# Streamed weight tiles of two kinds written at byte 192 of their buffers instead of byte 0

## The chip, the cores and the metric

The kernel runs on one core of one Trainium2 chip. The metric is device time in microseconds (us) of one execution. Before the change the median of 3 runs is 396.92 us (396.71 to 397.27).

## The reference

Two layers of a decoder trunk, batch 1, 256 rows of 1024 features, float32. Cut to what matters here:

```
for l in range(2):
    h = rms_norm(x, norm_g[l])
    proj = h @ w_in[l]                       # 1024 -> 10 groups of 512 columns
    q_a, k_a, v_a, q_h, f_h, i_h, q_m, z = split(proj)
    o_a = moba_attention(rope(norm(q_a)), rope(norm(k_a)), v_a)
    o_h = rms_norm(hgrn2_chunkwise(q_h, f_h, i_h, lb[l]))
    kv_m = rms_norm(mem, mem_norm_g[l]) @ w_mem_kv[l]      # 1024 -> 2 * 512 columns
    o_m = memory_attention(norm(q_m), norm(k_m), v_m)
    y = concat(o_a, o_h, o_m) * silu(z)
    x = x + y @ w_out[l]                     # 1536 -> 1024
```

The three kinds of large product (`h @ w_in`, `mem @ w_mem_kv`, `y @ w_out`) are nearly all of the arithmetic.

## The kernel before

**One stream of weights.** The weights of both layers come as 120 chunks of 128 partitions x 1024 float32 in a fixed list (`chunks`). For each chunk SyncE loads the raw tile `wr` (4 buffers); ScalarE writes `wh`, a copy in fp32r, the reduced 4-byte matmul format (`h_to`, line 143, or line 148 with a gain for the memory chunks; 4 buffers); VectorE writes the rest `wl` = `wr` - `wh` (`l_to`, line 158 or 161; 3 buffers). Activations are split into a high and a low part in the same way (`hTh`, `hTl` in the tile `hT`; `mTh`, `mTl`; `yh`, `yl`), and each product is made of three matmuls: high x high, high x low and low x high. `slot` asks for loads, high parts and low parts a set number of chunks ahead of TensorE. Small work (norms, attention, the recurrence) runs as generators that `step` moves on between the pieces of a group; its matmuls stand between the large ones on TensorE.

**Four kinds of chunk.** In a name such as `acc<-wh,hT` the profile puts the moving operand (the one that streams through TensorE) ahead of the stationary one (the one that a weight load, PEld, puts in place). In this document one matmul with its weight load is a step.

- "B" chunks, the row-output groups KA, QA, IH, ZH, QM and VA (`group_b`): the weights are the moving operand, 512 wide, and a 128x128 block of `hT` is stationary. 6 groups x 8 blocks of the depth x 2 row halves x 3 products x 2 layers = 576 steps.
- "K" chunks, the memory projections (`group_kv`): the same form with `mTh` or `mTl` stationary. 2 column halves x 8 x 2 x 3 x 2 layers = 192 steps (one of them is cut in two).
- "A" chunks in `group_a`, the column-output groups FH, QH, ZA and ZM: a 128x128 block of weights is stationary and `hT` is the moving operand, 256 wide. 768 steps.
- "A" chunks in `w_out_phase` (line 1213): weights stationary, `yh` or `yl` moving, 256 wide. 576 steps.

In each layer the order is K (layer 0: ahead of all; layer 1: right behind the output projection of layer 0), FH, QH (A), KA, QA, IH, ZH (B), ZA, ZM (A), QM, VA (B), then the output projection. So TensorE goes over from 512-wide steps to 256-wide ones and back several times in a layer.

**Where the tiles start.** Buffers of `wh` and `wl` are 1088 elements (4352 bytes, 17 x 256) wide, and 1024 elements of them are used. The first one used is number 16 (byte 64) for A chunks and number 0 for B and K chunks. In the built program all these buffers start at multiples of 256 bytes. Start bytes of matmul operands within a stretch of 256 bytes:

| steps | moving operand | stationary operand |
|---|---|---|
| A (`group_a`) | `hT`: 0 | `wh`, `wl`: 64 |
| output projection | `yh`, `yl`, `y`: 0 | `wh`, `wl`: 64 |
| B | `wh`, `wl`: 0 | `hT`: 0 |
| K | `wh`, `wl`: 0 | `mTh`, `mTl`: 0 |
| scores of the memory attention (line 1142, told as L198) | `kmh`, `kml`: 64 | `qmh`: 64, `qml`: 0 |

All large steps are recorded by the helper `mm` (line 198), so they are told apart by their tiles.

Of the kernel before, what the change touches and what calls it, by code (L numbers as in the profile page):

```python
# [46 lines left out]
def hymba_kernel(ctx: ExitStack, tc: tile.TileContext, front, x, x_t, mem, mem_t, positions, w_in, w_out, w_mem_kv,  # L47
# [40 lines left out]
    chunks = []  # L88
# [30 lines left out]
    def pin(ins):  # L119
        tc.keep_in_program_order(ins)  # L120
# [12 lines left out]
    def parts(i):  # L133
        return (slice(0, 512), slice(512, 1024)) if i < 3 else (slice(0, 1024),)

    def h_to(n):
        while st["h"] < min(n, len(chunks)):
            i = st["h"]
            off = 16 if chunks[i][0] == "A" else 0
            whs[i] = sb.tile([128, 1088], F32R, name="wh", tag="wh", bufs=WH_BUFS)[:, off:off + 1024]  # L140
            g = chunks[i][2]
            if g is None:
                ins = nc.scalar.copy(whs[i], raws[i])  # L143
                if i == 12:
                    pin(ins)
            else:
                for sl in parts(i):
                    nc.scalar.activation(whs[i][:, sl], raws[i][:, sl], AF.Copy, scale=gT[:, g:g + 1])  # L148
            st["h"] += 1

    def l_to(n):
        while st["l"] < min(n, len(chunks)):
            i = st["l"]
            off = 16 if chunks[i][0] == "A" else 0
            wls[i] = sb.tile([128, 1088], F32R, name="wl", tag="wl", bufs=WL_BUFS)[:, off:off + 1024]
            g = chunks[i][2]
            if g is None:
                nc.vector.tensor_tensor(wls[i], raws[i], whs[i].bitcast(F32), op=OP.subtract)  # L158
            else:
                for sl in parts(i):  # L160
                    nc.vector.scalar_tensor_tensor(wls[i][:, sl], in0=raws[i][:, sl], scalar=gT[:, g:g + 1],  # L161
                                                   in1=whs[i][:, sl].bitcast(F32),
                                                   op0=OP.mult, op1=OP.subtract)
            st["l"] += 1
# [24 lines left out]
    def slot(first):  # L189
        if first:  # L190
            c = st["c"]
            dma_to(c + 1 + DMA_AHEAD)
            h_to(c + 1 + H_AHEAD)
            l_to(c + 1 + L_AHEAD)
        step()
# [163 lines left out]
    m_split(0, 1)  # L359
    m_split(1, 2)  # L360
    h_to(1)
    l_to(1)
    h_to(2)
    l_to(2)

    rm = cst.tile([128, 2], F32, name="rm")
# [993 lines left out]
```

## Time and profile before

| | us |
|---|---|
| median of 3 runs (lowest, highest) | 396.92 (396.71, 397.27) |
| the profiled execution | 397.62 |
| its span in the trace | 395.8 |

The profiled execution is 1.8 us longer than its span, and 0.7 us above the median of the runs. The page gives the busy time of each engine, the chain of work that ended last, and groups of equal instructions with their busy time, the mean duration of one in ns and the idle time ahead of them. Durations of matmuls overlap, since they are pipelined; the pace is read from the start times of the timeline.

### The profile page before, as it was taken

What the parts mean: (1) busy time and instruction counts of PE and PEld (TensorE: products, weight loads), DVE (VectorE), ACT (ScalarE), POOL (GpSimd) and SP (SyncE); (2) the same over time, 40 slices, a digit from 0 to 9 for tenths busy, and PEclk for the clock granted to TensorE, in tenths of its full rate; (3) what the DMA queues carried; (4) which work ended last, traced back from release to release, by engine and by line L of the source; (5) the groups of instructions that cost most, each with busy time, mean ns of one, the idle gap of its engine ahead of it and who ended that gap; (6) DMA issues with size and microseconds to landing.
All of it is one profiled execution on the core that took longest, in us unless ns stands there. A gap on an engine that the chain in (4) does not pass through costs nothing.

```text
span 395.8 us, 7904 instructions
## 1 busy us (share of the span) xinstructions
PE 391.1 (99%) x3051; PEld 354.0 (89%) x3051; DVE 315.5 (80%) x628; ACT 249.6 (63%) x399; POOL 65.9 (17%) x94
## 2 busy tenths in 40 slices
PE   8999999999999999999999999999999999999996
PEld 5889988888999888999988999888889998899996
DVE  4699988999899848776586998699989695588553
ACT  6787765455959679644463775444696774977330
POOL 2005923650002002000061030042200100200000
PEclk9999999999999999999999999999999999999999
DMA  7998664368634454433646475464764346344203
GB/s 251 421 357 270 206 214 159 121 197 265 206 122 157 161 178 139 155 115 111 209 162 209 124 237 185 152 201 172 206 221 154 113 134 214 133 159 161 87 21 108
DMA packets 22662, 70.92 MB, mean 179 GB/s; under 512 B 2529, under 2 KB 5985, under 8 KB 22625
## 3 DMA queue, kind: packets, MB, share of 16 engines
q1 hardware_dynamic: 19872, 67.86, 50.8%
q10 hardware_dynamic: 2752, 2.56, 2.4%
q8 instruction: 24, 0.39, 0.4%
q14 instruction: 14, 0.11, 0.1%
HBM read 67.27 MB, written 1.05 MB: 173 GB/s over the span
## 4 chain that ended last, share of the span: by engine, by line
PE 98%; DMA 1%; SPq 0%; ACT 0%; DVE 0%; issue 0%; DVEq 0%
PE acc L198 61%; PE acc L1213 17%; PE sd L198 11%; PE sd L202 2%; PE sd L1087 1%; PE sd L1066 1%; DMA wr<-in_front_dram 1%; PE sd L981 1%; PE sd L1175 1%; PE sd L765 0%; PE sd L633 0%; PE sd L1121 0%; SPq L123 0%; ACT wh L148 0%; PE sd L423 0%; PE sd L460 0%
## 5 line engine op out<-in xcount | busy, mean ns | idle before, releaser
L143 ACT CAST wh<-wr 128x1024 fp32r<-128x1024 f32 x104 | 108.8, 1052 | 82.6 <-PE acc L198 45.9
L158 DVE TENSOR_TENSOR wl<-wr,wh 128x1024 fp32r<-128x1024 f32 x104 | 126.5, 1221 | 26.8 <-PE acc L1213 8.5
L198 PE MATMUL acc<-wh,hT 128*128 128x512 f32 x384 | 120.5, 392 | 0.0
L198 PE MATMUL acc<-hT,wh 128*128 128x256 f32 x512 | 91.1, 279 | 0.0
L198 PEld LDWEIGHTS acc<-wh,hT 128*128 128x128 f32 x384 | 72.0, 188 | 14.8
L198 PEld LDWEIGHTS acc<-hT,wh 128*128 128x128 f32 x512 | 78.1, 188 | 0.3
L198 PE MATMUL acc<-wl,hT 128*128 128x512 f32 x192 | 75.6, 394 | 0.0
L198 PE MATMUL acc<-hT,wl 128*128 128x256 f32 x256 | 70.9, 279 | 0.0
L198 PEld LDWEIGHTS acc<-hT,wl 128*128 128x128 f32 x256 | 48.1, 189 | 0.2
L198 PEld LDWEIGHTS acc<-wl,hT 128*128 128x128 f32 x192 | 36.1, 188 | 7.2
L1213 PE MATMUL acc<-yh,wl 128*128 128x256 f32 x128 | 35.7, 279 | 0.0
L1213 PE MATMUL acc<-yh,wh 128*128 128x256 f32 x128 | 35.5, 281 | 0.0
L1213 PE MATMUL acc<-yl,wh 128*128 128x256 f32 x128 | 35.4, 278 | 0.0
L1213 PEld LDWEIGHTS acc<-yl,wh 128*128 128x128 f32 x128 | 24.1, 189 | 0.1
L161 DVE SCALAR_TENSOR_TENSOR wl<-wr,gT,wh 128x1024 fp32r<-128x1024 f32 (+1 forms) x14 | 19.1, 1374 | 6.4 <-ACT wh L148 2.1
L1213 PEld LDWEIGHTS acc<-yh,wl 128*128 128x128 f32 x128 | 24.1, 188 | 0.0
L1213 PEld LDWEIGHTS acc<-yh,wh 128*128 128x128 f32 x128 | 24.0, 188 | 0.1
L148 ACT ACTIVATE wh<-wr,gT 128x1024 fp32r<-128x1024 f32 (+1 forms) x14 | 15.2, 1090 | 11.7 <-PE acc L198 3.6
L1213 PE MATMUL acc<-y,wh 128*128 128x256 f32 x128 | 21.8, 276 | 0.0
L1213 PEld LDWEIGHTS acc<-y,wh 128*128 128x128 f32 x128 | 19.2, 188 | 0.0
L1047 ACT ACTIVATE P<-P,nba,rq 128x256 f32<-128x256 f32 (+1 forms) x32 | 17.2, 539 | 0.9 <-DVE nba L1038 0.8
L1213 PE MATMUL acc<-y,wl 128*128 128x256 f32 x64 | 17.5, 276 | 0.0
(245 smaller groups left out, 667.5 us busy)
## 6 DMA issues: line engine op xcount, KB each, us to landing
wr<-in_w_in_dram SPq DMA_DIRECT2D x80, 512.0 KB, 3.7
wr<-in_w_out_dram SPq DMA_DIRECT2D x24, 512.0 KB, 3.2
wr<-in_w_mem_kv_dram SPq DMA_DIRECT2D x12, 512.0 KB, 3.3
k<-k ACTq DMA_DIRECT2D x8, 256.0 KB, 4.1
zT<-in_x_dram SPq DMA_DIRECT2D x2, 512.0 KB, 8.9
xs<-in_x_t_dram SPq DMA_DIRECT2D x2, 512.0 KB, 9.9
memr<-in_mem_dram SPq DMA_DIRECT2D x2, 512.0 KB, 5.7
mw<-in_front_dram SPq DMA_DIRECT2D x2, 384.0 KB, 5.8
```

The costliest lines, as they stand in the source:

```text
L143: ins = nc.scalar.copy(whs[i], raws[i])
L148: nc.scalar.activation(whs[i][:, sl], raws[i][:, sl], AF.Copy, scale=gT[:, g:g + 1])
L158: nc.vector.tensor_tensor(wls[i], raws[i], whs[i].bitcast(F32), op=OP.subtract)
L161: nc.vector.scalar_tensor_tensor(wls[i][:, sl], in0=raws[i][:, sl], scalar=gT[:, g:g + 1], in1=whs[i][:, sl].bitcast(F32), op0=OP.mult, op ...
L198: nc.tensor.matmul(o, lhsT=a, rhs=b, start=s, stop=e)
L202: tc.keep_in_program_order(nc.tensor.matmul(o, lhsT=a, rhs=b, start=True, stop=True))
L981: nc.tensor.transpose(pt[:, p * 128:(p + 1) * 128], kr[:, t, p * 128:(p + 1) * 128], ident)
L1047: pin(nc.scalar.activation(P[:, i, kc[t]], P[:, i, kc[t]], AF.Exp, bias=nb[:, c:c + 1], scale=rq[:, r:r + 1], accum_out=sm[:, c:c + 1]))
L1066: pin(nc.tensor.transpose(pt[:, i * 128:(i + 1) * 128], P[:, i, bs], ident))
L1087: pin(nc.tensor.matmul(po[w][rows, c + o:c + 256], lhsT=va[:, b, h * 64:(h + 1) * 64], rhs=PT[e][:, p, 256 * b:256 + 128 * b], start=b == ...
L1175: nc.tensor.transpose(pt[:, i * 256 + t * 128:i * 256 + (t + 1) * 128], P[:, t, i, b * 128:(b + 1) * 128], ident)
L1213: ins = nc.tensor.matmul(a, lhsT=wt, rhs=y, start=first and (to is not None or b % 2 == 0), stop=n == nk - 1 and j == 2, skip_group_check= ...
```

## The change

The offset into the buffer becomes 48 elements (byte 192) for B and K chunks; A chunks keep 16 (byte 64). Buffers, their sizes and their addresses are as before, and so is every instruction on every engine and its order: only the addresses that ScalarE and VectorE write to, and TensorE reads its moving operand from, are 192 bytes higher in the 48 B and 16 K chunks.

```
 def h_to(n):
...
-            off = 16 if chunks[i][0] == "A" else 0
+            off = 16 if chunks[i][0] == "A" else 48
             whs[i] = sb.tile([128, 1088], F32R, name="wh", tag="wh", bufs=WH_BUFS)[:, off:off + 1024]
...
 def l_to(n):
...
-            off = 16 if chunks[i][0] == "A" else 0
+            off = 16 if chunks[i][0] == "A" else 48
             wls[i] = sb.tile([128, 1088], F32R, name="wl", tag="wl", bufs=WL_BUFS)[:, off:off + 1024]
```

In the table of start bytes the moving operand of B and K steps goes from 0 to 192. Counted round a stretch of 256 bytes, the stationary operand then starts 64 bytes further on than the moving one in B and K steps, as it does in A steps and the output projection.

More of the change, by code (lines that the diff above doesn't have):

```diff
@@ L138, in h_to @@
             i = st["h"]
-            off = 16 if chunks[i][0] == "A" else 0
+            off = 16 if chunks[i][0] == "A" else 48
             whs[i] = sb.tile([128, 1088], F32R, name="wh", tag="wh", bufs=WH_BUFS)[:, off:off + 1024]
@@ L153, in l_to @@
             i = st["l"]
-            off = 16 if chunks[i][0] == "A" else 0
+            off = 16 if chunks[i][0] == "A" else 48
             wls[i] = sb.tile([128, 1088], F32R, name="wl", tag="wl", bufs=WL_BUFS)[:, off:off + 1024]
```

## The prediction

> **What bounds the kernel now.** I read the page's busy times and its chain first, then what TensorE waited for.
>
> ```profile
> span 395.8 us, 7904 instructions
> PE 391.1 (99%) x3051; PEld 354.0 (89%) x3051; DVE 315.5 (80%) x628; ACT 249.6 (63%) x399; POOL 65.9 (17%) x94
> PE 98%; DMA 1%; SPq 0%; ACT 0%; DVE 0%; issue 0%; DVEq 0%
> PE acc L198 <- ACT wh L148: 0.9, 1, 0.9
> PE sd L198 <- PEq L1349: 0.8, 1, 0.8
> ```
>
> TensorE is busy for 391.1 of 395.8 us, the chain runs through it for 98%, and it waits 1.7 us in all for others. So the time is the sum of the steps of TensorE, and an edit counts by what it does to the distance from one step's start to the next. Durations of steps overlap and don't tell that distance; the timeline does. First the A steps (256 wide, weights stationary) in two places of layer 0, with the last 512-wide step ahead of the first place:
>
> ```profile
> 28.30 0.40 PE L198 MATMUL acc<-wl,mTh 128*128 128x512 f32 x1
> 28.53 0.28 PE L198 MATMUL acc<-hT,wl 128*128 128x256 f32 x1
> 28.65 0.40 PE L198 MATMUL acc<-hT,wh 128*128 128x256 f32 x2
> 28.89 0.28 PE L198 MATMUL acc<-hT,wl 128*128 128x256 f32 x1
> ...
> 29.95 0.28 PE L198 MATMUL acc<-hT,wl 128*128 128x256 f32 x1
> ```
>
> ```profile
> 46.00 0.28 PE L198 MATMUL acc<-hT,wl 128*128 128x256 f32 x1
> 46.12 0.39 PE L198 MATMUL acc<-hT,wh 128*128 128x256 f32 x2
> 46.34 0.28 PE L198 MATMUL acc<-hT,wl 128*128 128x256 f32 x1
> ...
> 47.36 0.28 PE L198 MATMUL acc<-hT,wl 128*128 128x256 f32 x1
> ```
>
> Each triple (high x high, low x high, high x low) has one `hT,wl` step, so four triples, 12 steps, lie between the outer rows. The first place takes 29.95 - 28.53 = 1.42 us for them, 118.3 ns a step; the second 47.36 - 46.00 = 1.36 us, 113.3 ns. The instructions and the start bytes of their operands are the same. I call these the slow pace and the settled pace; the slow one costs 5.0 ns a step. How long each lasts is seen by counting steps in windows of equal length:
>
> ```profile
> 28.60:43.20 14.60, 14.60 (x126) 1.00 0.82 269
> 222.60:237.20 14.60, 14.60 (x131) 1.00 0.64 203
> 295.10:303.80 8.70, 8.70 (x77) 1.00 0.44 151
> 312.00:320.70 8.70, 8.70 (x79) 1.00 0.38 122
> 352.90:360.20 7.30, 7.30 (x64) 1.00 0.38 129
> 182.90:190.20 7.30, 7.30 (x66) 1.00 0.49 162
> ```
>
> The columns are the window, TensorE's busy time with the steps in brackets, the granted clock and the DMA share and rate. The clock is full everywhere, and the DMA share is highest in one slow window (0.82) and low in another (0.44), so neither sets the pace. The slow windows are the first, third and fifth. Now the 512-wide B steps, where the A steps of QH end:
>
> ```profile
> 51.55 0.40 PE L198 MATMUL acc<-wh,hT 128*128 128x512 f32 x1
> 51.79 0.40 PE L198 MATMUL acc<-wl,hT 128*128 128x512 f32 x1
> ...
> 53.17 0.39 PE L198 MATMUL acc<-wl,hT 128*128 128x512 f32 x1
> ...
> 54.53 0.39 PE L198 MATMUL acc<-wl,hT 128*128 128x512 f32 x1
> ```
>
> From 53.17 on, six steps take 1.36 us, 226.7 ns a step: twice the settled pace of the half as wide A step. The six ahead of them take 53.17 - 51.79 = 1.38 us, and the first takes 51.79 - 51.55 = 0.24 us in place of 0.227. So a B stretch has no lasting slow pace, but an entry from A steps costs about 0.02 + 0.01 = 0.03 us.
>
> **What goes with the slow pace.** It begins where a 512-wide step is followed directly by a 256-wide one. The rows at 28.30 and 28.53 are one such place. The others that the timeline shows:
>
> ```profile
> 99.07 0.40 PE L198 MATMUL acc<-hT,wh 128*128 128x256 f32 x2
> 99.31 0.28 PE L198 MATMUL acc<-hT,wl 128*128 128x256 f32 x1
> ...
> 100.02 0.28 PE L198 MATMUL acc<-hT,wl 128*128 128x256 f32 x1
> 293.55 0.28 PE L198 MATMUL acc<-hT,wl 128*128 128x256 f32 x1
> 293.67 0.40 PE L198 MATMUL acc<-hT,wh 128*128 128x256 f32 x2
> 293.91 0.28 PE L198 MATMUL acc<-hT,wl 128*128 128x256 f32 x1
> 347.74 0.28 PE L1213 MATMUL acc<-yh,wh 128*128 128x256 f32 x1
> ...
> 348.68 0.28 PE L1213 MATMUL acc<-yh,wl 128*128 128x256 f32 x1
> ```
>
> ```profile
> 154.55 0.28 PE L1213 MATMUL acc<-yh,wh 128*128 128x256 f32 x1
> ...
> 155.37 0.28 PE L1213 MATMUL acc<-yl,wh 128*128 128x256 f32 x1
> ```
>
> Six steps take 0.71 us at 99.31 (118.3 ns) and three 0.36 at 293.55 (120). At 347.74 and 154.55, where VA gives way to the output projection, it is 8 steps in 0.94 us (117.5) and 7 in 0.82 (117.1). I read it so: the weight load of the next step runs beside the moving stream of this one, the two keep step with each other, and a pair of streams can settle into a good or a bad relation. In B steps both streams start at byte 0, in A steps the stationary one starts 64 bytes further on. A relation that suits the one is carried into the other as a bad one, and holds until other work breaks it.
>
> **The change, part by part.** *Writing at byte 192.* Nothing moves on any engine; the 64 chunks are written to other addresses. A chunks are already written at byte 64, so the trace has both. The summary of a window in which A chunks are written (28 to 42 us), then of one with B chunks (66 to 76 us); durations are ns, lowest/median/highest:
>
> ```profile
> L143 ACT CAST wh<-wr x6: 1042/1053/1056, 28.8 to 39.9; 128x1024 fp32r<-128x1024 f32 x6
> L158 DVE TENSOR_TENSOR wl<-wr,wh x6: 1211/1219/1226, 27.1 to 39.6; 128x1024 fp32r<-128x1024 f32 x6
> L143 ACT CAST wh<-wr x3: 1053/1058/1058, 66.5 to 71.9; 128x1024 fp32r<-128x1024 f32 x3
> L158 DVE TENSOR_TENSOR wl<-wr,wh x2: 1214/1214/1215, 71.0 to 73.0; 128x1024 fp32r<-128x1024 f32 x2
> ```
>
> The medians differ by 5 ns both ways: nothing at byte 64, and I take nothing for byte 192. Were it 5 ns for each of the 128 writes, 0.6 us would lie on ScalarE and VectorE, which are busy 63% and 80% and for which TensorE waits 0.9 us once, so it would stay beside the matmuls. Without that cover it would be the 0.6 us.
>
> *Going over to A steps.* With 192 in place of 0, stationary less moving start is 64 bytes (round 256) in all large steps. I expect the relation to be carried over as a good one. Gains: at 28.53, the windows hold 126 against 131 steps, 5 x 113.3 ns = 0.57 us. From 295.1, 77 against 79, 2 x 113.3 = 0.23 us, where 5.0 ns on each of the 77 steps says 0.39; I take 0.39, since whole steps are a coarse count. The short pieces at 99.07, 154.5 and 347.74 have about 9 steps each: 27 x 5.0 = 0.13 us. The stretch in the output projection (64 against 66 steps, 0.23 us by count, 64 x 5.0 = 0.32) comes after matmuls of the memory attention, whose operands keep their addresses: nothing taken, 0.3 us kept for the lower end.
>
> *Going over to B and K steps.* By the order of the groups there are five entries straight from 256-wide steps (QH to KA and ZM to QM in both layers, and the output projection of layer 0 to K), at 0.03 us: 0.15 us gone. Inside B stretches nothing is gained, since 226.7 ns is the settled pace.
>
> *Sum.* 0.57 + 0.39 + 0.13 + 0.15 = 1.24 us. The profiled execution would go from 397.62 to 396.4, and the median, 0.7 us lower, from 396.92 to 395.7. All of it lies on the path, as TensorE is the path. What is late next: ScalarE and VectorE have to make weights 0.3% faster, and their idle time of 37% and 20% allows it.
>
> The price of the B steps themselves at byte 192 is not in the trace. Its bounds: settled (0), or the excess of steps with a moving operand that starts away from byte 0. The scores of the memory attention are such steps (`kmh`, `kml` at byte 64):
>
> ```profile
> 159.38 0.28 PE L198 MATMUL sd<-kmh,qmh 128*128 128x256 f32 x1
> ...
> 161.15 0.28 PE L198 MATMUL sd<-kmh,qmh 128*128 128x256 f32 x1
> ```
>
> Between them lie 15 steps in 1.77 us, 118.0 ns, 4.7 above the settled pace. On 768 B and K steps that is 3.6 us. I take 0, because the settled rows nearest in kind, the A steps, have the same 64 bytes between their streams; the 4.7 ns stay for the range. A gain below the settled pace I leave out: no row of a 256-wide or 512-wide fp32r stretch goes below 113.3 or 226.7 ns.
>
> **A rule against it.** The slow pace, 118.3 against 113.3 ns with equal addresses, is the row. The Trainium skill, page TensorE: Matmul & The Clock Gate, section Step-by-step: what each phase is for, says that TensorE has two independent SBUF read ports, one for the stream and one for weight loads, so that loading the next weights takes no read bandwidth from the running matmul. By it no start byte matters and the sum would be 0. The trace neither bears this out nor refutes it: a stretch is slow beside an equal one that isn't, but no row has one kind of step at two start bytes.
>
> **The rivals.** *No change.* The pace is set by how instructions follow each other at a change of width, not by addresses. For it: equal addresses run at both paces, and other breaks decide too. Against it: nearly all slow stretches start at the one kind of place where the start bytes differ. Then the 1.24 us stay and the time is 396.9. The rule of the Trainium skill on two read ports (page TensorE: Matmul & The Clock Gate) would lead here. A change in which some entries settle and others fall into the slow pace by chance also ends within 0.8 us of this.
>
> *Slower: the moving operand's own start.* It is the start of the moving operand that has to be at byte 0, as it is in every settled stretch quoted, and not its distance from the stationary one. Place: the 768 B and K steps. Price: 4.7 ns each, 3.6 us, so 400.5 if the A entries stay as they are, and 399.3 if these gain too. It decides from 1.24 / 0.0047 = 264 slow steps of 768 on. For it: the scores of the memory attention. Against it: they stand in short pieces between other work and change their stationary start from step to step (`qmh` 64, `qml` 0), so they never get to settle.
>
> **How the numbers follow.** A measurement of this kernel can tell about 0.2%, 0.8 us, from no change. I give the forecast 0.50, no change 0.28, slower 0.22. The likeliest is 395.7. The gains go from the long stretch and little else (0.57 + 0.15, about 0.8 us, 396.1) to the 1.24 us with the output projection's 0.3 and, as an estimate, another 0.6 if the B steps that follow other work (some 20 places) also start settled at 0.03 us each: 2.2 us, 394.7. With a little for a profile that is one execution, the low end is 394.4. The case of no change reaches to 397.7. Of the slower case I take in what begins at 398.2, and leave out most of it, 0.17. Faster by over 0.2% 0.50, within 0.28, slower by over 0.2% 0.22.
>
> **What would show it.** Right: from 28.53 on, 12 A steps in 1.36 us and 131 steps in the first window; the same at 99, 293 and 347; B steps at 1.36 us for six, and no extra 0.03 us at 51.55. Wrong: the slow pace still there behind the 512-wide steps (no change), or six B steps taking 1.39 us (4.7 ns each) all through a group (slower). A cast or subtraction of B chunks that takes more than 1058 or 1226 ns would show that writing has a price. The forecast as a whole falls if the A stretches settle and the time doesn't follow, since then TensorE wasn't the bound.

## The result and the profile after

The changed kernel takes 400.76 us (median of 5 runs, 400.25 to 400.93) against 397.0 (396.71 to 397.43): ratio 1.0088, 95% interval 1.0075 to 1.0101 (the two medians alone make 1.0095, inside the interval). It is slower by about 3.8 us where 1.2 us less was forecast.

The page's head and TensorE's only wait, after:

```profile
span 398.2 us, 7904 instructions
PE 394.4 (99%) x3051; PEld 353.6 (89%) x3051; DVE 315.3 (79%) x628; ACT 250.0 (63%) x399; POOL 65.8 (17%) x94
PE 99%; DVE 0%; DVEq 0%; issue 0%
PE sd L198 <- PEq L1349: 0.8, 1, 0.8
```

TensorE is the path as before, and is busy for 3.3 us more in a span that is 2.4 us longer: the 0.9 us that it waited for the first high part in the profile of before are not there in this execution.

The A steps behind the memory chunks of layer 0, after (they began at 28.53 before), and the same window of A steps, after and then before:

```profile
27.93 0.62 PE L198 MATMUL acc<-wl,mTh 128*128 128x512 f32 x2
28.39 0.28 PE L198 MATMUL acc<-hT,wl 128*128 128x256 f32 x1
...
28.74 0.28 PE L198 MATMUL acc<-hT,wl 128*128 128x256 f32 x1
...
29.76 0.28 PE L198 MATMUL acc<-hT,wl 128*128 128x256 f32 x1
```

```profile
28.60:42.50 13.90, 13.90 (x125) 1.00 0.85 270
```

```profile
28.60:42.50 13.90, 13.90 (x120) 1.00 0.81 262
```

The first triple takes 0.35 us, and then nine steps take 1.02 us, 113.3 ns a step. The stretch is settled, with 125 steps in place of 120. So this half of the forecast came true. The B steps of one group, before and then after; between the two rows lie 32 steps in both:

```profile
66.45 0.39 PE L198 MATMUL acc<-wl,hT 128*128 128x512 f32 x1
...
73.70 0.39 PE L198 MATMUL acc<-wl,hT 128*128 128x512 f32 x1
```

```profile
66.80 0.39 PE L198 MATMUL acc<-wl,hT 128*128 128x512 f32 x1
...
74.27 0.39 PE L198 MATMUL acc<-wl,hT 128*128 128x512 f32 x1
```

7.25 us were 226.6 ns a step; 7.47 us are 233.4, that is 6.7 ns more. B steps no longer settle, for as long as the stretch lasts. The groups of the page show it as a longer mean duration, 397 and 399 ns against 392 and 394:

```profile
L198 PE MATMUL acc<-wh,hT 128*128 128x512 f32 x384 | 122.6, 397 | 0.0
L198 PE MATMUL acc<-wl,hT 128*128 128x512 f32 x192 | 76.5, 399 | 0.0
```

Writing at byte 192 costs nothing, as forecast: the medians are 1049 and 1216 ns, against 1058 and 1214 before (the window of B chunks, 66 to 76 us, after):

```profile
L143 ACT CAST wh<-wr x3: 1048/1049/1052, 66.1 to 71.7; 128x1024 fp32r<-128x1024 f32 x3
L158 DVE TENSOR_TENSOR wl<-wr,wh x3: 1216/1216/1217, 70.3 to 75.7; 128x1024 fp32r<-128x1024 f32 x3
```

**Where the time went.** For every step of the trace I take the distance to the next step's start, less the settled pace (226.67 or 113.33 ns), and add it up by kind; distances over 20 ns too long are breaks and stand apart. B and K steps together: 0.79 us before, 4.85 after, 4.06 us lost (4.85 us over 768 steps are 6.3 ns a step). A steps: 1.20 before, 0.26 after, 0.94 us gained. Breaks in K, at the start of the kernel above all: 1.68 before, 0.93 after, 0.75 us that this execution had less. Together 4.06 - 0.94 - 0.75 = 2.4 us, the difference of the two spans. Without the start, which differs between executions, it is 3.1 us of the 3.76 between the medians; the profiled execution after (400.25 us) is the lowest of its five runs and that of before was above its median; the other 0.6 may come from that, which no run shows.

### The profile page after: what moved, and what is told of

Same layout as the page of the kernel before. It is cut to its first block, busy times and chain, and to the rows that moved or that the text cites. A ratio compares the mean times of both kernels' runs of the same rounds, so it can differ in the third digit from the quotient of the medians.

```text
span 398.2 us, 7904 instructions
## 1 busy us (share of the span) xinstructions
PE 394.4 (99%) x3051; PEld 353.6 (89%) x3051; DVE 315.3 (79%) x628; ACT 250.0 (63%) x399; POOL 65.8 (17%) x94
## 3 DMA queue, kind: packets, MB, share of 16 engines
HBM read 67.27 MB, written 1.05 MB: 172 GB/s over the span
## 4 chain that ended last, share of the span: by engine, by line
PE 99%; DVE 0%; DVEq 0%; issue 0%
PE acc L198 62%; PE acc L1213 17%; PE sd L198 13%; PE sd L202 2%; PE sd L1087 1%; PE sd L1066 1%; PE sd L981 1%; PE sd L1175 1%; PE sd L1121 0%; PE sd L765 0%; PE sd L633 0%; PE sd L423 0%; PE sd L460 0%; DVE xs L1248 0%; DVEq L1356 0%
## 5 line engine op out<-in xcount | busy, mean ns | idle before, releaser
L198 PE MATMUL acc<-wh,hT 128*128 128x512 f32 x384 | 122.6, 397 | 0.0
L198 PE MATMUL acc<-wl,hT 128*128 128x512 f32 x192 | 76.5, 399 | 0.0
```

The lines of the kernel that those rows point to most:

```text
L198: nc.tensor.matmul(o, lhsT=a, rhs=b, start=s, stop=e)
```

## The experiments

In all kernels the instructions and their order are those of before, and only start bytes differ (in e1 and e2 `hT`, `mTh` and `mTl` are also made 256 bytes longer, to have room for the shift). "Distance" is the stationary operand's start less the moving one's, round 256 bytes. Theory 1 is the rival of the prediction (the moving operand's own start has to be at byte 0); theory 2 says that the distance decides whether steps settle, and that 512-wide steps want another one than 256-wide ones.

The sums over the settled pace, by the rule above, and the times against the kernel before. For e1 to e11 each ratio is to executions of the kernel before that were taken beside them; their medians are 397.26 to 397.54 us. The sums are those of one execution each.

| kernel | B and K distance | B, K us over | A distance | A us over | ratio (95% interval) |
|---|---|---|---|---|---|
| before | 0 | 0.79 | 64 | 1.20 | |
| the change | 64 | 4.85 | 64 | 0.26 | 1.0088 (1.0075 to 1.0101) |
| e1 all moved by 192 | 0 | 0.68 | 64 | 1.23 | 1.0008 (0.9998 to 1.0017) |
| e2 `hT`, `mT` at 64 | 64 | 4.88 | 64 | 1.33 | 1.0126 (1.0099 to 1.0153) |
| e3 B, K at 256 | 0 | 0.80 | 64 | 0.65 | 0.9997 (0.9986 to 1.0008) |
| e4 last of each at 192 | 0, 6 chunks 64 | 1.13 | 64 | 0.83 | 0.9997 (0.9985 to 1.0009) |
| e5 B, K at 64 | 192 | 1.99 | 64 | 0.27 | 1.0017 (1.0007 to 1.0026) |
| e6 B, K at 128 | 128 | 4.40 | 64 | 1.38 | 1.0098 (1.0083 to 1.0114) |
| e7 A at 0 | 0 | 0.78 | 0 | 4.88 | 1.0101 (1.0087 to 1.0114) |
| e8 5 chunks at 192 | 0, 5 chunks 64 | 1.09 | 64 | 0.26 | 0.9984 (0.9976 to 0.9993) |
| e9 K alone at 192 | B 0, K 64 | 1.86 | 64 | 0.64 | 1.0012 (1.0002 to 1.0021) |
| e10 B alone at 192 | B 64, K 0 | 3.79 | 64 | 0.81 | 1.0063 (1.0049 to 1.0076) |
| e11 5 chunks at 64 | 0, 5 chunks 192 | 1.05 | 64 | 0.28 | 0.9979 (0.9970 to 0.9989) |

**e1: both operands moved by 192 bytes.**

```
 off = {"A": 0, "B": 48, "K": 48, "W": 16}[chunks[i][0]]   # W: the output projection's chunks
...
-    mTh = sb.tile([128, 8, 256], F32R, name="mTh")
+    mTh = sb.tile([128, 2112], F32R, name="mTh")[:, 48:2096].rearrange("p (k s) -> p k s", k=8)
...
-    hT = sb.tile([128, 8, 2, 256], F32R, name="hT")
+    hT = sb.tile([128, 4160], F32R, name="hT")[:, 48:4144].rearrange("p (k c s) -> p k c s", k=8, c=2)
```

`mTl` is changed like `mTh`.

> Both operands of the large projection steps are moved by the same 192 bytes: B and K weights at byte 192, hT, mTh and mTl also at byte 192, and the weights of the A steps at byte 256, so that each pair keeps the distance that it has in the kernel before (0 for B and K, 64 for A). The output projection is left alone. Theory 1 (the moving operand's own start has to be at byte 0 of 256): B and K steps at about 233 ns as after the change, and A steps slow too, near 118 ns, since hT moves at byte 192; time over 401 us. Theory 2 (the distance between stationary and moving start counts: 0 is good for 512-wide steps, 64 for 256-wide ones): B and K settle at 226.7 ns, A at 113.3 with the slow stretches of before; time 397.0 us.

**e2: the same distance as after the change, but with the moving operand of B and K at byte 0.** As e1 with `hT`, `mTh` and `mTl` at element 16, and:

```
 off = {"A": 32, "B": 0, "K": 0, "W": 16}[chunks[i][0]]
```

> The other way to 64 bytes between the streams: B and K weights stay at byte 0 as the moving operand, and hT, mTh and mTl go to byte 64; the weights of the A steps go to byte 128 so that their distance stays 64. Theory 1 (own start of the moving operand): B and K settle at 226.7 ns, A steps (hT moves at byte 64) slow near 118 ns, time about 400.6 us. Theory 2 (distance): B and K at about 233 ns as after the change, A settled at 113.3, time about 400.7 us. The total hardly tells them apart, the pace of each kind in the trace does.

The same B group, e1 (31 steps between the rows) and e2 (32 steps):

```profile
66.34 0.39 PE L198 MATMUL acc<-wl,hT 128*128 128x512 f32 x1
...
73.36 0.39 PE L198 MATMUL acc<-wl,hT 128*128 128x512 f32 x1
```

```profile
66.94 0.39 PE L198 MATMUL acc<-wl,hT 128*128 128x512 f32 x1
...
74.41 0.39 PE L198 MATMUL acc<-wl,hT 128*128 128x512 f32 x1
```

e1: 7.02 us, 226.5 ns a step with the moving operand at byte 192. e2: 7.47 us, 233.4 ns with it at byte 0. Theory 1 has all A steps slow in both kernels, since `hT` moves at 192 or 64: 768 steps at 118 ns would be 3.6 us over. They are no slower in sum than before (1.23 and 1.33 us over). Theory 1 falls. The time of e1 says the same, 397.63 us, no change that can be told; that of e2, 401.78, is slower under either theory.

The A sums hide a shift that theory 2 did not foresee. It had expected the slow stretches of before in e1 and settled A steps in e2. Instead, the stretch behind the memory chunks of layer 0 is settled in both (in e1 behind a break like that of e3 below), and later stretches that were settled before are slow. Two windows of e2, then the window of the kernel before that answers to the second one (97 steps, where e2 has 94):

```profile
28.60:42.50 13.90, 13.90 (x125) 1.00 0.80 260
314.10:324.90 10.80, 10.80 (x94) 1.00 0.28 99
```

```profile
311.00:321.80 10.80, 10.80 (x97) 1.00 0.31 99
```

So e2, with the same distances as the change in A, B and K steps, does not have its A gain in the end (1.33 against 0.26 us over): it settles behind the memory chunks, and grows slow further on, behind other work. Why it does so with `hT` moved is not shown.

**e3: byte 256.**

```
 off = {"A": 16, "B": 64, "K": 64, "W": 16}[chunks[i][0]]
```

> B and K weights written at byte 256 of their buffers in place of 0 or 192. Theories 1 and 2 both: start and distance are 0 again counted round 256, so 397.0 us with settled B and K steps at 226.7 ns. If what costs is any offset into the buffer (a longer row, the last bytes of the buffer), it stays near 400.8 us.

396.91 us, no change. It isn't an offset as such, nor the end of the buffer. Its A sum is lower than before (0.65), though all distances are those of before. The place, e3:

```profile
27.62 0.39 PE L198 MATMUL acc<-wl,mTh 128*128 128x512 f32 x1
27.95 0.38 PE L198 MATMUL acc<-hT,wl 128*128 128x256 f32 x1
...
28.41 0.28 PE L198 MATMUL acc<-hT,wl 128*128 128x256 f32 x1
...
29.44 0.28 PE L198 MATMUL acc<-hT,wl 128*128 128x256 f32 x1
```

The step ahead of the A steps takes 0.33 us, 0.1 us too long. Behind this break the stretch settles by itself (nine steps in 1.03 us). So a break can also decide whether a stretch is slow.

**e4: only the last chunk ahead of each change to 256-wide steps at byte 192.**

```
 off = 48 if i in (7, 31, 47, 67, 91, 107) else (16 if chunks[i][0] == "A" else 0)
```

> Of B and K chunks only the last one ahead of a 256-wide group is written at byte 192 (6 of 64 chunks, 72 steps); all others stay at byte 0. If the relation of the streams is carried from the last 512-wide steps into the A steps, these are settled from 28.5 us on, and in the later places: 0.9 us gained as after the change, against 72 steps at 6 ns, 0.4 us lost, so about 396.5 us. If the A stretches settle after the change for another reason (the whole K group), nothing is gained and 0.4 us lost: 397.4 us.

397.31 us, no change: the expected gain was not there. The A steps behind ZH in layer 0 (slow before, 0.71 us for the six from 99.31), and a later A window, which held 123 steps before, in e4:

```profile
98.38 0.28 PE L198 MATMUL acc<-hT,wl 128*128 128x256 f32 x1
...
98.72 0.28 PE L198 MATMUL acc<-hT,wl 128*128 128x256 f32 x1
...
99.06 0.28 PE L198 MATMUL acc<-hT,wl 128*128 128x256 f32 x1
```

```profile
222.60:236.35 13.75, 13.75 (x119) 1.00 0.70 211
```

The entry behind ZH now settles (0.34 us for each of two triples), but the stretch behind the memory chunks of layer 1, settled before, is slow: 119 steps. There two shorter matmuls (384 and 128 wide) and a break lie at the change of width, so the relation isn't handed on directly. The A steps behind the memory chunks of layer 0 are settled in e4 too, but this execution has a break there as e3 has, so that place can't be put down to the one chunk.

**e5 and e6: bytes 64 and 128.**

```
 off = {"A": 16, "B": 16, "K": 16, "W": 16}[chunks[i][0]]    # e5; e6: B and K 32
```

> B and K weights at byte 64, hT, mTh and mTl at 0 as before: the stationary operand starts 192 bytes further on than the moving one (round 256). After e1 and e2 the distance is what counts. Theory 2a (512-wide steps settle at distance 0 alone): near 233 ns a step, about 401 us. Theory 2b (distance 64 is the bad one): 226.7 ns, 397.2 us.

> B and K weights at byte 128, distance 128. Theory 2a: near 233 ns a step, about 401 us. Theory 2b: 226.7 ns, 397.2 us.

32 B steps each, e5 and e6:

```profile
66.67 0.39 PE L198 MATMUL acc<-wl,hT 128*128 128x512 f32 x1
...
73.99 0.39 PE L198 MATMUL acc<-wl,hT 128*128 128x512 f32 x1
```

```profile
66.76 0.40 PE L198 MATMUL acc<-wl,hT 128*128 128x512 f32 x1
...
74.23 0.40 PE L198 MATMUL acc<-wl,hT 128*128 128x512 f32 x1
```

e5: 228.8 ns; e6: 233.4. Over all B and K steps the sums are 2.6 ns a step (1.99 us / 768) at distance 192 and 5.7 at 128, against 6.3 at 64 and 1.0 at 0, where it is entries alone. Neither form of theory 2 that I had written down fits: of the four distances only 0 settles, but 192 costs less than half of the others. The A steps behind them differ as well, though their own distance is 64 in both: after B and K steps at 192 they settle (0.27 us over), after 128 they don't (1.38).

**e7: the weights of the A steps at byte 0.**

```
 off = {"A": 0, "B": 0, "K": 0, "W": 16}[chunks[i][0]]
```

> The weights of the A steps (group_a alone, not the output projection) at byte 0 in place of 64, so that distance 0 holds for B, K and A; B and K as before. If 256-wide steps don't settle at distance 0: 118 ns on all 768, of which about 1.2 us are already there, so 2.4 us more, 399.6 us. If the distance only has to be the same on both sides of a change of width: the A stretches settle everywhere, 1.2 us less, 396.0 us.

e7, the A steps behind the memory chunks:

```profile
28.57 0.28 PE L198 MATMUL acc<-hT,wl 128*128 128x256 f32 x1
...
29.65 0.28 PE L198 MATMUL acc<-hT,wl 128*128 128x256 f32 x1
```

Nine steps in 1.08 us, 120.0 ns. All A steps are slow (4.88 us over, 6.4 ns a step): 401.25 us, where 399.6 was expected, since the price is 6.4 ns and not 4.7. It is no use to have the same distance on both sides of a change of width, since 256-wide steps don't settle at 0. This is the mirror image of the change. It isn't byte 0 as such: in e1 these weights start at byte 0 too, with `hT` at 192, and the stretch from 220.7 us on settles (138 steps, 0.2 ns over on average).

**e8 and e11: five chunks alone.** As e4 without chunk 67, the last memory chunk of layer 1; e11 at byte 64.

```
 off = 48 if i in (7, 31, 47, 91, 107) else (16 if chunks[i][0] == "A" else 0)   # e11: 16 if i in ...
```

> As e4, but without the last memory chunk of layer 1, whose A stretch is settled before anyway and got slow in e4: 5 chunks at byte 192, 60 steps at 6 ns (0.36 us) against 0.9 us in the A stretches. If relations are carried over as e4 shows, 0.4 to 0.6 us less than before, 396.7; if the start of the A stretch at 28 us is settled by something else than the carried relation, 397.2 or more.

> As e8, the same 5 chunks, at byte 64 in place of 192, since e5 had B steps at byte 64 only about 2.3 ns over the settled pace and its A stretches settled too. 60 steps x 2.3 = 0.14 us lost in place of 0.36, the same 0.9 us gained: 396.4, 0.7 us or so below before. If a single chunk is too short for this relation to form, the A stretches stay slow: 397.4.

e8, the window that was slow in e4:

```profile
222.60:236.35 13.75, 13.75 (x124) 1.00 0.66 210
```

124 steps: settled again, and so are the stretches behind the five chunks (A sum 0.26 us). 396.6 us for e8, 0.16% less than before, and 396.59 for e11, 0.21% less, each a median of 11 executions. Both intervals lie below 1: both kernels are a little faster than the kernel before, and so than the change. The five chunks cost 0.30 (e8) and 0.26 us (e11) in the B and K sum. That e11 beats e8 lies within their intervals.

**e9 and e10: the two parts of the change alone.**

```
 off = {"A": 16, "B": 0, "K": 48, "W": 16}[chunks[i][0]]    # e9; e10: B 48, K 0
```

> One part of the change alone: the memory chunks (K) at byte 192, B at 0. Theory 2 (distance 64 costs a 512-wide step 6.3 ns for good, and its relation settles the 256-wide steps behind it): 192 steps x 5.5 to 6.3 ns = 1.1 to 1.2 us lost, 0.57 us gained in the A stretch from 28.5 us on, so 0.6 us over before, near 397.9. If the parts are not independent, another sum than e9 + e10 = the change.

> The other part alone: the row-output chunks (B) at byte 192, K at 0. Theory 2: 576 x 6.3 = 3.6 us, less the 0.6 us of entry costs that B has before, less about 0.5 us in the A stretches behind B: 2.5 us over before, near 399.8. With e9 the sum is near the 3 to 3.8 us of the whole change.

The A window behind the memory chunks, then one behind ZH in layer 1; first e9, then e10:

```profile
30.00:43.50 13.50, 13.50 (x121) 1.00 0.78 265
296.50:305.00 8.50, 8.50 (x75) 1.00 0.40 142
```

```profile
29.00:42.50 13.50, 13.50 (x117) 1.00 0.79 265
298.50:307.00 8.50, 8.50 (x77) 1.00 0.38 125
```

With K at 192 the first window settles (121 steps) and the second stays slow (75); with B at 192 it is the other way round (117, 77; counted from the start of the second stretch, at 296.6 and 297.7 us, it is 75 and 77 as well). Each part settles the A steps right behind it and no others. 397.99 and 399.98 us, near what was expected; the ratios add up to 1.0075, the lower end of the interval of the whole change. The sums add up better: 1.07 + 3.00 = 4.07 us lost in B and K steps and 0.56 + 0.39 = 0.95 us gained in A steps, against 4.06 and 0.94 for the whole change.

## Why the prediction was wrong

- *TensorE's pace is the time*: right. The sums by kind account for the difference of the spans.
- *Writing at byte 192 costs nothing*: right, 1049 and 1216 ns.
- *Going over to A steps settles them*: right in place and nearly in size. Of the 0.57 + 0.39 + 0.13 = 1.09 us forecast, 1.00 lie in A steps of `group_a` and 0.09 in two short pieces of the output projection; 0.94 us were measured in the A steps, and the output projections lost 0.03 of their sum (0.66 to 0.63). The slow pace is 4.4 to 4.5 ns too long when the starts are read to the ns, not 5.0, so the stretch from 295 us held 0.32 us and not 0.39. The reading behind it has two parts. That the steps ahead of a direct change of width decide the pace behind it is borne out by e9 and e10, where each part settles what follows it, and by e8 and e11, where a few chunks ahead of the change are enough. That it takes the same distance on both sides is refuted: A steps at 64 also settle behind B and K steps at 192 (e5, e11), and behind the change they are handed a good pace by 512-wide steps that don't settle themselves. The prediction had the place right for a reason that doesn't hold, which is luck in part.
- *Going over to B and K steps, 0.15 us less*: void, since these steps have no settled pace any more to be late for.
- *The B and K steps at byte 192 cost 0*: this step failed, and it turned the sign. It rested on "the settled rows nearest in kind, the A steps, have the same 64 bytes between their streams". They are not near in this: 512-wide steps settle at distance 0 and run 6.3 ns late at 64 (the change, e2), 256-wide ones settle at 64 and run 6.4 ns late at 0 (e7). A distance can't be carried from one width to the other. The bound of 4.7 ns, kept for the range, was the right kind of cost and a quarter too small: 6.3 ns a step over all 768, entries included, and 6.7 inside a stretch.
- *The slower rival* had the place, the sign and nearly the time (400.5, or 399.3 with the A gains), but its mechanism is refuted: e1 has the moving operand at byte 192 and settles, e2 has it at byte 0 and doesn't. That its 400.5 came near is luck: its price was too small (3.6 us against 4.06 lost) and it left out A gains of 0.94 us that were there, and the two errors offset in part.
- *The range* ended at 398.2 on the judgement that the slower case had 0.22. The profile had no row of a 512-wide step at another distance than 0. With nothing measured on either side of that price, the settled case should not have had more than twice the chance of the other.
- *The rule of the Trainium skill* (page TensorE: Matmul & The Clock Gate, section Step-by-step: what each phase is for) that stream and weight loads have independent read ports: the prediction concluded from it that start bytes make no difference. Here they make one of about 3% (512-wide) and 6% (256-wide) of a step with the same instructions in the same order (e2 and e7 against before), so that conclusion does not hold for these fp32r steps. Whether the rule itself fails is not shown, since no run shows the ports.

**What stays open.** Why these distances: that the two reads get in each other's way would fit, but no run shows the reads themselves. Why 192 ahead of A steps settles them and 128 doesn't, and why A stretches further on grow slow in e1 and e2, is open too. Distances 128 and 192 of the 256-wide steps were not tried, nor other steps than 64 bytes. The slow stretches in the output projection of layer 1 stayed in all kernels (the sum for the output projections of both layers is 0.63 to 0.68 us in every trace); they follow the memory attention, whose operands were not moved.

## What to carry to other kernels

Where TensorE is the path and each step brings its own weight load, look at the distance between the start bytes of the moving and the stationary operand, for each width of step apart, and at the pace from start to start, which the page's durations hide. A distance that is good for one width says nothing of another, so try it for each kind alone before it is made uniform. A slow stretch that begins at a change of kind can be ended by the few steps ahead of the change: there five chunks did what all 64 were moved for, at 0.3 us lost in place of 4.1.

## What was not expected of the hardware

- fp32r steps of the same form and the same addresses ran at two paces for 100 steps and more, 113.3 and 118 ns, and which one was settled at the entry or by a break of 0.1 us (before against e3, e9 against e10).
- 512-wide steps over the settled 226.7 ns, by distance, as means over all steps with their entries: 0 none but at entries, 192 2.6 ns, 128 5.7 ns, 64 6.3 ns. 256-wide steps over 113.3 ns: 64 none or 4.7 ns, 0 6.4 ns.
